# Dilated attention scores: the low part of q over 128 rows, and the sink mixer's outputs parked in DRAM

## The chip, the cores and the metric

The kernel runs on one core of one Trainium2 chip. The metric is the time of one execution on the device in microseconds; the time of a version is the median of several runs. The profile is that of one execution, taken by the hardware profiler.

## What is computed

Two layers of a decoder over 512 tokens of width 1024. Each layer projects the normalized row once and feeds three causal token mixers: sparse attention (A: an indexer scores the keys, the best 128 are kept), dilated window attention (B), and sliding-window attention with sinks (C). Their outputs are gated, merged and projected, and a feed-forward block of width 4096 follows. The part that the change touches is B's scores and C's outputs:

```
for g, (window, dil) in enumerate(((128, 1), (512, 4), (2048, 16))):     # B, four heads in each group
    pos    = t[:, None] - dil * arange(window // dil + 1)[None, :]
    logits = einsum('bqhd,bqkhd->bqhk', q_g, k_g[:, pos]) * scale         # masked where pos < 0
    ...                                                                   # softmax, values, merged by denominators
o_c    = sink_window_attention(...)                                       # C, eight heads, 128 tokens back
merged = g0 * (o_a @ w_a) + g1 * (o_b @ w_b) + g2 * (o_c @ w_c)
```

Everything is float32. Heads have 64 dimensions, tokens come in four blocks of 128.

## The kernel before

TensorE multiplies in a reduced float32 form, so each operand x is split into a high part (x rounded to that form) and a low part (x minus the high part), and a product is the sum of three: high by high, high by low, low by high. `mm3` (lines 287 to 289) issues these three for the big products. `load` fetches a stretch of weights on SP's queue into a buffer `raw`, ScalarE casts the high part (line 263), VectorE or GpSimd subtracts for the low part (line 264).

In the scores the three products are folded into two matmuls, because a head has 64 dimensions and the array 128 rows. In mixers A and C `stack_q` puts the high part of q on 64 rows and the low part on the other 64; `dup_k` holds k twice, and `qk` (lines 368 and 369) multiplies over 128 rows both times. Mixer B stores it the other way: for each head `e` of a pair the tile of k holds the high part on the head's own 64 rows and the low part on the other 64; the tile of q holds the high part on both. So one matmul over 128 rows (line 701) gives high by high plus high by low, and a second one over the head's own 64 rows only (line 702) adds low by high. That low part of q (`ql`) takes one row half per head, two heads in one tile.

`b_project(pr)` projects v, q and k for a pair of heads of each of the three groups, in chunks of 384 columns, token block by token block. After the rope turn a deferred step `post` (the post, below) transposes the block on TensorE and evacuates it: for each head ScalarE copies the high part to the own half (line 660) and, for q, to the other half (line 663), then VectorE subtracts for the low part (line 666). There is one such pair of copies for group 0 (64x128) and one for groups 1 and 2 (64x256).

`b_attend(pr)` then runs eight units of scores, softmax and values as a pipeline: two heads, two kinds (group 0, or groups 1 and 2), two halves of the token blocks. A unit of the second kind has eight matmuls of 128 columns in its scores. One of the first kind has four: two of 128 and two of 256 columns in the first half of the tokens, four of 256 in the second. Line 727 on VectorE takes the row's extreme, line 732 on ScalarE the exponential.

In each layer the program orders the work thus: projections for A and C, the indexer's scores, `c_attend` side by side with gate products, `b_project(0)`, `b_attend(0)` side by side with gate products, `b_project(1)`, `b_attend(1)` in the same way, A's projection with the merge of B, `a_attend` with the rest of the gates, then `split_o` (all mixer outputs into high and low part), `branches`, the output projection and the feed-forward block. The steps of the top-k selection on VectorE (lines 508 and 509) are spread over the dilated mixer's stages. The gates' values are stored in DRAM when they are made (line 849) and fetched in `branches`.

The framework sets the final order on each engine: its planner goes through the instructions with an estimate of each one's cost and of when its inputs are due, and places a tile in a buffer when one is free. Big tiles of 4 KB per partition share the pool `arena` of 15 buffers. The outputs `oC` of C occupy two of them from `c_attend` to `split_o`.

Of the kernel before, what the change touches and what calls it, by code (L numbers as in the profile page):

```python
# [22 lines left out]
P = 128  # L23
T = 512
# [19 lines left out]
class Trunk:  # L44
# [81 lines left out]
        return inv  # L126

    def rope_turns(self, pos, inv):
        """negated angles of rope, reduced to turns in [-0.5, 0.5], and the same a quarter turn on;
        a step for each vector instruction"""  # L130
        v = self.nc.vector
        n = NT * 32
        keep = lambda dt=F32: self.arena([P, n], dt)
        posf = self.cp.tile([P, NT], F32, name="posf")
        yield v.tensor_copy(posf, pos)
        ang = keep()
        yield v.tensor_tensor(
            ang.rearrange("p (b d) -> p b d", d=32), inv.unsqueeze(1).to_broadcast([P, NT, 32]),
            posf.unsqueeze(2).to_broadcast([P, NT, 32]), op=ALU.mult)
        whole = keep(I32)  # L140
        yield v.tensor_copy(whole, ang)
        parts = self.arena([P, 4, n], I32)
        yield v.tensor_scalar(parts[:, 0, :], whole, 255, None, op0=ALU.bitwise_and)
        for j in (1, 2):
            yield v.tensor_scalar(parts[:, j, :], whole, 8 * j, 255, op0=ALU.arith_shift_right, op1=ALU.bitwise_and)
        yield v.tensor_scalar(parts[:, 3, :], whole, 24, None, op0=ALU.arith_shift_right)
        pf = self.arena([P, 4, n], F32)
        yield v.tensor_copy(pf, parts)
        wf = keep()
        yield v.tensor_copy(wf, whole)  # L150
        s1, s2 = keep(), keep()
        yield v.tensor_tensor(s2, ang, wf, op=ALU.subtract)
        yield v.tensor_scalar(s2, s2, float(np.float32(1 / (2 * math.pi))), None, op0=ALU.mult)
        inv2pi = Fraction(INV_2PI_NUM, 1 << 160)
        for j in range(4):
            c = (inv2pi * (1 << (8 * j))) % 1
            c1 = Fraction(round(c * (1 << 14)), 1 << 14)
            p = pf[:, j, :]
            if j == 0:
                yield v.tensor_scalar(s1, p, float(c1), None, op0=ALU.mult)  # L160
            else:
                yield v.scalar_tensor_tensor(s1, p, float(c1), s1, op0=ALU.mult, op1=ALU.add)
            yield v.scalar_tensor_tensor(s2, p, float(np.float32(float(c - c1))), s2, op0=ALU.mult, op1=ALU.add)
        near = keep()

        def turn_back(x):
            """x -> (nearest whole number) - x"""
            yield v.tensor_scalar(near, x, ROUND, None, op0=ALU.add)
            yield v.scalar_tensor_tensor(x, near, ROUND, x, op0=ALU.subtract, op1=ALU.subtract)

        yield from turn_back(s1)
        yield v.tensor_tensor(s1, s2, s1, op=ALU.subtract)
        yield from turn_back(s1)
        q = keep()
        yield v.tensor_scalar(near, s1, 0.25, None, op0=ALU.is_gt)
        yield v.scalar_tensor_tensor(q, s1, 0.25, near, op0=ALU.add, op1=ALU.subtract)
        self.turns = (s1, q)
# [10 lines left out]
            nc.scalar.activation(self.cos[:, :, h * 32 : h * 32 + 32], s2v, AF.Sin, scale=two_pi)  # L188

    def square_sum(self, h, half):  # L190
        """sum over a half of the row, with half of D * EPS"""
        nc = self.nc
        ss = self.st([P, 1], "st")
        junk = self.st([P, T], "sg")
        nc.scalar.activation(junk, h[:, half * T : half * T + T], AF.Square, accum_out=ss)
        if half == 0:
            nc.vector.tensor_scalar(ss, ss, D * EPS, None, op0=ALU.add)
        return ss
# [9 lines left out]
        return rs  # L208

    def norm(self, h, gb, ss0=None):  # L210
        """yields the halves of the normalized row"""
        nc = self.nc
        rs = self.inv_rms(h, ss0)
        yield
        for half in range(2):
            u = self.st([P, T], "t")
            s = slice(half * T, half * T + T)
            nc.vector.scalar_tensor_tensor(u, h[:, s], rs, gb[:, s], op0=ALU.mult, op1=ALU.mult)
            yield u
# [21 lines left out]
        yield  # L241

    def norm_T(self, *args):
        """the normalization up to its transposes; those wait for `catch_up`"""
        g = self.norm_T_steps(*args, late=True)
        next(g)
        next(g)
        self.late.append(g)
# [4 lines left out]
        self.late = []  # L253

    def load(self, parts, width, lo_eng=None):
        """parts: list of (dst slice fn, src ap); one staged tile of `width` f32 columns."""
        nc = self.nc
        raw = self.st([P, 1024], "raw")
        for dst, src in parts:
            nc.sync.dma_start(dst(raw), src)  # L260
        hi = self.st([P, 1024], "hi", F32R)
        lo = self.st([P, 1024], "lo", F32R)
        nc.scalar.copy(hi[:, :width], raw[:, :width])  # L263
        (lo_eng or nc.vector).tensor_tensor(lo[:, :width], raw[:, :width], f32(hi[:, :width]), op=ALU.subtract)  # L264
        return hi, lo

    def load_chunk(self, w, k0, nk, cols, pool_tiles=()):
        """rows k0*128.. of w, column runs `cols` [(start, n)] side by side -> per k (hi, lo) APs."""
        n = sum(c for _, c in cols)
        out = []  # L270
        for k in range(k0, k0 + nk, 2):
# [36 lines left out]
            yield  # L308

    def rope(self, src, tb, nh, dup=1):  # L310
        """src [P, nh*64] (psum or sbuf) -> sbuf tile [P, nh, dup, 64]"""
        nc = self.nc
        x = src.rearrange("p (h two d) -> p h two d", two=2, d=32)
        c = self.cos[:, tb : tb + 1, :].to_broadcast([P, nh, 64])
# [22 lines left out]
        return ps  # L337

    def stack_q(self, roped, nh):
        """[tok, nh*64] -> [P = (hi 64 | lo 64), nh, tok]"""  # L340
        nc = self.nc
        q = self.arena([P, 8, P])[:, :nh, :]
        np_ = nh // 2
        ps = self.transposes(roped, np_)
        for e in range(2):
            src = ps[e * 64 : e * 64 + 64, :np_, :]
            hi = q[0:64, e::2, :]
            nc.scalar.copy(hi, src)
            nc.vector.tensor_tensor(q[64:128, e::2, :], src, f32(hi), op=ALU.subtract)  # L349
        return q  # L350

    def dup_k(self, roped, n, tb, dst):
        """roped [tok, n*128] (each key head twice) -> dst[i][P, hi/lo, 512]"""
        nc = self.nc
        ps = self.transposes(roped, n)
        for i in range(n):
# [12 lines left out]
        nc.tensor.matmul(out, q, k[:, 1, c0 : c0 + n], start=False, stop=True)  # L369

    def softmax(self, ps_list, masks, n, init=None, sink=None, normalize=True):
        """each psum [P, n] -> exp in an sbuf tile [P, heads, n]"""
        nc = self.nc
        nh = len(ps_list)
        lg = self.st([P, 1024], "lg")
# [31 lines left out]
        return pt  # L407

    def av_shared(self, pts, vs, n):
        """sum over blocks of stacked v^T P^T -> psum [P, n]; rows 64.. are the low parts"""  # L410
        nc = self.nc
        ps = self.psum([P, T], "o")
        for i, (pt, v) in enumerate(zip(pts, vs)):
# [2 lines left out]
        return ps  # L416

    def put_o(self, ps, heads, qb, oT):
        """oT(pair) -> [P, 512] f32 AP; heads: list in psum column order"""
        nc = self.nc  # L420
        n = len(heads) * P
        t = self.st([P, T], "t")
# [2 lines left out]
            o = oT(hd // 2)[(hd % 2) * 64 : (hd % 2) * 64 + 64, qb * P : (qb + 1) * P]  # L425
            nc.vector.tensor_tensor(o, ps[0:64, i * P : (i + 1) * P], t[0:64, i * P : (i + 1) * P], op=ALU.add)

# [1 line left out]
    def idx_project(self, uT, w, wk=None):  # L429
        self.iq = {}  # L430

# [136 lines left out]

        yield from pipeline([unit(qb, h0) for qb in range(NT) for h0 in (0, 3)])

# [1 line left out]
    def c_project(self, uT, w):  # L572
        self.cq = {}

# [10 lines left out]
    def c_attend(self, l):  # L585
# [41 lines left out]
            return logits, rest, transpose, values  # L627

        yield from pipeline([unit(qb, g) for qb in range(NT) for g in range(2)])

# [1 line left out]
    def b_alloc(self):  # L632
        self.stat_n = self.st([P, 2, NT, 4], "bst", bufs=6)
        self.stat_c = self.st([P, 2, NT, 4], "bst", bufs=6)
# [1 line left out]
    def b_project(self, uT, w, pr):  # L636
        nc = self.nc
        res = {}
        for which, off in (("v", OFF_BV), ("q", OFF_BQ), ("k", OFF_BK)):
            cols = [(off + g * 256 + pr * P, P) for g in range(3)]  # L640
            if which != "v":
# [1 line left out]
                both = [self.arena([P, 2, T]) for _ in range(2)]  # L643
                res[which] = [[full[:, e, :] for e in range(2)]] + [[both[e][:, g, :] for e in range(2)] for g in range(2)]
                if which == "q":
                    lo0, lo12 = self.arena([P, 2, T])[:, 0, :], self.arena([P, 2, T])
                    res["ql"] = [lo0, lo12[:, 0, :], lo12[:, 1, :]]

                def ev(tb, ps, which=which, full=full, both=both):
                    r = self.rope(ps[:, :384], tb, 6)  # L650
# [3 lines left out]
                    def post():  # L654
                        pt = self.transposes(r, 3)
                        src = pt[:, 0, :], pt[:, 1:3, :].rearrange("p g (j r) -> p g r j", r=4)
                        for e in range(2):
# [3 lines left out]
                            if which == "q":  # L661
                                for x, dst in zip(src, (full[:, e, s], classes(both[e]))):
                                    nc.scalar.copy(dst[other], x[own])
                            low = (lo0[own, s], classes(lo12)[own]) if which == "q" else (full[other, e, s], classes(both[e])[other])
                            for x, dst, lo in zip(src, (full[:, e, s], classes(both[e])), low):
                                nc.vector.tensor_tensor(lo, x[own], f32(dst[own]), op=ALU.subtract)

                    return post
            else:
# [19 lines left out]
    def b_attend(self, pr):  # L689
# [6 lines left out]
        def unit(e, kind, b2, po):  # L696
# [2 lines left out]

            def qk(out, g, qs, ks):  # L700
                nc.tensor.matmul(out, r["q"][g][e][:, qs], r["k"][g][e][:, ks], start=True, stop=False)  # L701
                nc.tensor.matmul(out, r["ql"][g][ep, qs], r["k"][g][e][ep, ks], start=False, stop=True)  # L702

            st = self.stat_n if kind == 0 else self.stat_c
            bs = (2 * b2, 2 * b2 + 1)
# [115 lines left out]
            v.tensor_tensor(self.oB[:, pr, :], t, t2, op=ALU.add)  # L821
            yield

# [1 line left out]
    def split_o(self):  # L825
        nc = self.nc
        out = []
# [154 lines left out]


def pipeline(units):
    """units' stages drawn side by side, each unit one stage behind the one before it"""
    depth = len(units[0])
    for r in range(len(units) + depth - 1):
        for s in reversed(range(depth)):
# [7 lines left out]


def merge(*streams):
    """(generator, its number of steps) pairs, drawn evenly side by side"""
    order = sorted(((i + 0.5) / n, j) for j, (_, n) in enumerate(streams) for i in range(n))  # L1000
    for _, j in order:
        next(streams[j][0], None)
# [1 line left out]
def build(tr):  # L1004
# [53 lines left out]
    for l in range(DEPTH):  # L1058
# [29 lines left out]
        run(ba)  # L1088
        run(tk)
        merge((ap, 5), (tr.b_merge(), 5))  # L1090
        merge((tr.a_attend(), 11), (gt, 12))
        run(gt)
        tr.split_o()
        for f in range(NK):
# [60 lines left out]
```

## Time and profile before

| | |
|---|---|
| median of 3 runs | 1804.34 us (1802.95 to 1808.7) |
| span of the profiled execution | 1805.4 us |
| TensorE busy | 1755.3 us, 97% |
| VectorE busy | 1048.1 us, 58% |
| ScalarE busy | 817.9 us, 45% |
| mean granted TensorE clock | 0.995 of full speed |
| DMA | 186.32 MB, 103 GB/s on average |

The span reaches from the first to the last instruction of the profiled execution; no time of that execution beside its span is given. Busy shares are averages over stages with different limits. A matmul's recorded duration holds its latency, and successive ones overlap, so how fast they follow one another is read from their start times.

### The profile page before, as it was taken

What the parts mean: (1) busy time and instruction counts of PE and PEld (TensorE: products, weight loads), DVE (VectorE), ACT (ScalarE), POOL (GpSimd) and SP (SyncE); (2) the same over time, 40 slices, a digit from 0 to 9 for tenths busy, and PEclk for the clock granted to TensorE, in tenths of its full rate; (3) what the DMA queues carried; (4) which work ended last, traced back from release to release, by engine and by line L of the source; (5) the groups of instructions that cost most, each with busy time, mean ns of one, the idle gap of its engine ahead of it and who ended that gap; (6) DMA issues with size and microseconds to landing.
All of it is one profiled execution on the core that took longest, in us unless ns stands there. A gap on an engine that the chain in (4) does not pass through costs nothing.

```text
span 1805.4 us, 24273 instructions
## 1 busy us (share of the span) xinstructions
PE 1755.3 (97%) x8832; PEld 1483.2 (82%) x8832; DVE 1048.1 (58%) x2200; ACT 817.9 (45%) x1681; POOL 187.5 (10%) x163
## 2 busy tenths in 40 slices
PE   7999999999999999999999999999999999999998
PEld 6789889777879888888887798988788798888886
DVE  7986748667855333333488866596688443333333
ACT  5484544437434333424355845345383342424142
POOL 3310211221000000000021112021210000000000
PEclk9999999999999999999999999999999999999999
DMA  5323333331762322222332243332228422233321
GB/s 179 71 67 99 82 100 85 97 81 51 218 227 74 113 94 93 94 94 93 113 111 64 63 123 88 100 80 75 74 74 263 152 94 93 96 103 104 105 95 47
DMA packets 184344, 186.32 MB, mean 103 GB/s; under 512 B 16672, under 2 KB 125216, under 8 KB 184224
## 3 DMA queue, kind: packets, MB, share of 16 engines
q1 hardware_dynamic: 184224, 184.77, 34.3%
q8 instruction: 69, 1.13, 0.3%
q14 instruction: 51, 0.42, 0.1%
HBM read 165.82 MB, written 16.78 MB: 101 GB/s over the span
## 4 chain that ended last, share of the span: by engine, by line
PE 84%; DVE 9%; ACT 3%; issue 3%; DMA 1%; POOL 0%; SPq 0%; POOLq 0%; ACTq 0%; DVEq 0%
PE psg L287 24%; PE psg L289 24%; PE psg L288 24%; DVE t L324 2%; PE pst L336 1%; PE psl L702 1%; PE psl L701 1%; DVE a L492 1%; DVE a L349 1%; ACT lg L385 1%; PE pst L739 1%; PE pst L560 1%; PE psl L368 1%; ACT hi L263 1%; DVE t L320 1%
## 5 line engine op out<-in xcount | busy, mean ns | idle before, releaser
L263 ACT CAST hi<-raw 128x1024 fp32r<-128x1024 f32 (+3 forms) x320 | 295.6, 930 | 280.1 <-PE psg L289 221.2
L287 PE MATMUL psg<-uT,hi 128*128 128x512 f32 (+1 forms) x896 | 349.7, 390 | 0.0
L288 PE MATMUL psg<-uT,hi 128*128 128x512 f32 (+1 forms) x896 | 345.6, 386 | 0.0
L289 PE MATMUL psg<-uT,lo 128*128 128x512 f32 (+1 forms) x896 | 344.9, 385 | 0.0
L264 DVE TENSOR_TENSOR lo<-raw,hi 128x1024 fp32r<-128x1024 f32 (+4 forms) x237 | 267.8, 1140 | 115.9 <-ACT hi L263 110.6
L287 PE MATMUL psg<-hi,a 128*128 128x512 f32 x640 | 249.8, 390 | 1.8 <-ACT a L876 1.8
L289 PE MATMUL psg<-hi,a 128*128 128x512 f32 x640 | 249.3, 390 | 0.0
L288 PE MATMUL psg<-lo,a 128*128 128x512 f32 x640 | 249.0, 389 | 0.0
L264 POOL TENSOR_TENSOR lo<-raw,hi 128x768 fp32r<-128x768 f32 (+2 forms) x83 | 160.9, 1954 | 615.6 <-ACT hi L263 502.7
L288 PE MATMUL psg<-lo,uT 128*128 128x384 f32 (+2 forms) x624 | 219.1, 351 | 2.3 <-POOL lo L264 1.2
L287 PE MATMUL psg<-hi,uT 128*128 128x384 f32 (+2 forms) x624 | 220.9, 355 | 0.1
L289 PE MATMUL psg<-hi,uT 128*128 128x384 f32 (+2 forms) x624 | 218.5, 350 | 0.0
L287 PEld LDWEIGHTS psg<-uT,hi 128*128 128x128 f32 x896 | 169.2, 189 | 32.5 <-issue 0.7
L289 PEld LDWEIGHTS psg<-uT,lo 128*128 128x128 f32 x896 | 169.4, 189 | 31.8
L288 PEld LDWEIGHTS psg<-uT,hi 128*128 128x128 f32 x896 | 169.4, 189 | 29.4 <-issue 0.7
L947 DVE TENSOR_TENSOR a<-a,psg 128x512 f32<-128x512 f32 x64 | 43.9, 685 | 176.5 <-PE psg L289 176.5
L287 PEld LDWEIGHTS psg<-hi,a 128*128 128x128 f32 x640 | 120.1, 188 | 27.4 <-ACT a L876 2.6
L289 PEld LDWEIGHTS psg<-hi,a 128*128 128x128 f32 x640 | 120.1, 188 | 25.9 <-DVE a L877 0.9
L288 PEld LDWEIGHTS psg<-lo,a 128*128 128x128 f32 x640 | 120.2, 188 | 24.7
L910 DVE TENSOR_TENSOR a<-t,a 128x512 fp32r<-128x512 f32 x64 | 44.2, 690 | 153.3 <-ACT a L909 153.3
L288 PEld LDWEIGHTS psg<-lo,uT 128*128 128x128 f32 x624 | 117.7, 189 | 10.4 <-DVE lo L264 2.2
L287 PEld LDWEIGHTS psg<-hi,uT 128*128 128x128 f32 x624 | 117.7, 189 | 7.2 <-ACT uT L239 0.5
(195 smaller groups left out, 2502.0 us busy)
## 6 DMA issues: line engine op xcount, KB each, us to landing
raw<-in_w_in_dram SPq DMA_DIRECT2D x336, 128.0 KB, 2.8
raw<-in_w_up_dram SPq DMA_DIRECT2D x64, 512.0 KB, 4.8
raw<-in_w_down_dram SPq DMA_DIRECT2D x64, 512.0 KB, 4.8
raw<-in_w_in_dram SPq DMA_DIRECT2D x24, 512.0 KB, 4.7
sgd<-sg SPq DMA_DIRECT2D x48, 256.0 KB, 2.0
sg<-sgd SPq DMA_DIRECT2D x48, 256.0 KB, 3.7
raw<-in_w_o_dram SPq DMA_DIRECT2D x16, 512.0 KB, 4.1
a<-in_x_dram SPq DMA_DIRECT2D x8, 512.0 KB, 8.4
```

Source lines behind the costliest of these rows:

```text
L263: nc.scalar.copy(hi[:, :width], raw[:, :width])
L264: (lo_eng or nc.vector).tensor_tensor(lo[:, :width], raw[:, :width], f32(hi[:, :width]), op=ALU.subtract)
L287: nc.tensor.matmul(out, lh, rh, start=start, stop=False)
L288: nc.tensor.matmul(out, lh, rl, start=False, stop=False)
L289: nc.tensor.matmul(out, ll, rh, start=False, stop=stop)
L320: nc.vector.tensor_tensor(v1, src.rearrange("p (h d) -> p h d", d=64), c, op=ALU.mult)
L324: self.last_dve = nc.vector.tensor_tensor(v1, v1, v2, op=ALU.add)
L336: self.nc.tensor.transpose(ps[:, i, :], src[:, i * P : (i + 1) * P], self.ident)
L349: nc.vector.tensor_tensor(q[64:128, e::2, :], src, f32(hi), op=ALU.subtract)
L368: nc.tensor.matmul(out, q, k[:, 0, c0 : c0 + n], start=True, stop=False)
L910: nc.vector.tensor_tensor(a[:, 1, :], r, f32(a[:, 0, :]), op=ALU.subtract)
L947: nc.vector.tensor_tensor(hc, hc, ps, op=ALU.add)
```

## The change

The low part of q is stored like the high part, on both halves of the rows: `ql` now has a tile for each head (three tiles of the arena instead of two), VectorE subtracts into the head's own half as before, and ScalarE copies the result into the other half. The second matmul of `qk` in B contracts over all 128 rows of k's tile. So it also adds low by low, which was left out before.

At the end of `c_attend` the two tiles of `oC` are stored in DRAM on SP's queue. `c_reload`, called after five of the eleven steps of `a_attend`, takes two tiles of the arena anew and fetches them. The gates' steps are drawn in two halves of six around it.

```diff
@@ c_attend, at its end, and a new function
         yield from pipeline([unit(qb, g) for qb in range(NT) for g in range(2)])
+        self.oCd = []
+        for g in range(2):
+            d = self.dr.tile([P, 2, T], F32, name=self.uid("oCd"))
+            nc.sync.dma_start(d, self.oC[g])
+            self.oCd.append(d)
+
+    def c_reload(self):
+        self.oC = [self.arena([P, 2, T], F32) for _ in range(2)]
+        for g in range(2):
+            self.nc.sync.dma_start(self.oC[g], self.oCd[g])
@@ b_project
                 if which == "q":
-                    lo0, lo12 = self.arena([P, 2, T])[:, 0, :], self.arena([P, 2, T])
-                    res["ql"] = [lo0, lo12[:, 0, :], lo12[:, 1, :]]
+                    lfull = self.arena([P, 2, T])
+                    lboth = [self.arena([P, 2, T]) for _ in range(2)]
+                    res["ql"] = [[lfull[:, e, :] for e in range(2)]] + [[lboth[e][:, g, :] for e in range(2)] for g in range(2)]
...
-                            low = (lo0[own, s], classes(lo12)[own]) if which == "q" else (full[other, e, s], classes(both[e])[other])
+                            if which == "q":
+                                low = lfull[:, e, s], classes(lboth[e])
+                            else:
+                                low = full[:, e, s], classes(both[e])
                             for x, dst, lo in zip(src, (full[:, e, s], classes(both[e])), low):
-                                nc.vector.tensor_tensor(lo, x[own], f32(dst[own]), op=ALU.subtract)
+                                at = own if which == "q" else other
+                                nc.vector.tensor_tensor(lo[at], x[own], f32(dst[own]), op=ALU.subtract)
+                                if which == "q":
+                                    nc.scalar.copy(lo[other], f32(lo[own]))
@@ b_attend
                 nc.tensor.matmul(out, r["q"][g][e][:, qs], r["k"][g][e][:, ks], start=True, stop=False)
-                nc.tensor.matmul(out, r["ql"][g][ep, qs], r["k"][g][e][ep, ks], start=False, stop=True)
+                nc.tensor.matmul(out, r["ql"][g][e][:, qs], r["k"][g][e][:, ks], start=False, stop=True)
@@ build
-        merge((tr.a_attend(), 11), (gt, 12))
+        aa = tr.a_attend()
+        merge((aa, 5), (gt, 6))
+        tr.c_reload()
+        merge((aa, 6), (gt, 6))
```

The rest of the diff empties comments and docstrings.

## Rows read from the trace of the kernel before

**Rows 1.** The page, busy time: engine, us, share of the span, instructions.

```profile
PE 1755.3 (97%) x8832; PEld 1483.2 (82%) x8832; DVE 1048.1 (58%) x2200; ACT 817.9 (45%) x1681; POOL 187.5 (10%) x163
```

**Rows 2.** Stretches: bounds, length, busy time (instructions) per engine, clock, DMA share, GB/s.

```profile
core 0: us, PE busy (x) PEld busy (x) DVE busy (x) ACT busy (x) POOL busy (x), PEclk, DMA share, GB/s
172.00:190.00 18.00, 17.70 (x107) 17.30 (x106) 15.95 (x41) 11.51 (x33) 4.36 (x2) 1.00 0.40 96
...
206.00:240.00 34.00, 34.00 (x194) 27.12 (x194) 19.84 (x65) 16.73 (x43) 7.59 (x5) 1.00 0.39 102
...
300.00:316.00 16.00, 15.31 (x88) 14.30 (x86) 15.05 (x33) 6.43 (x19) 2.64 (x2) 1.00 0.18 45
316.00:332.00 16.00, 14.36 (x71) 11.21 (x72) 15.54 (x44) 7.12 (x22) 4.96 (x3) 1.00 0.37 100
332.00:366.00 34.00, 34.00 (x207) 27.64 (x207) 18.86 (x53) 16.93 (x41) 5.48 (x3) 1.00 0.28 82
...
412.00:450.00 38.00, 37.26 (x205) 31.47 (x204) 30.10 (x100) 30.16 (x75) 5.54 (x3) 1.00 0.17 53
...
1206.00:1222.00 16.00, 14.45 (x65) 11.15 (x66) 14.13 (x39) 6.48 (x20) 4.87 (x3) 0.89 0.39 101
```

**Rows 3.** Timeline of TensorE, dilated mixer: start, duration, line, rows*columns of weights, operand.

```profile
210.50 0.38 PE L702 MATMUL psl<-a,a 64*128 64x256 f32 x1
...
211.13 0.38 PE L702 MATMUL psl<-a,a 64*128 64x256 f32 x1
...
214.55 0.22 PE L288 MATMUL pso<-pt,a 128*64 128x128 f32 x1
214.61 0.22 PE L289 MATMUL pso<-pt,a 128*64 128x128 f32 x1
...
215.64 0.32 PE L702 MATMUL psl<-a,a 64*128 64x128 f32 x1
...
217.16 0.32 PE L702 MATMUL psl<-a,a 64*128 64x128 f32 x1
```

**Rows 4.** Timeline of TensorE: scores of the sink mixer, then of the indexer.

```profile
109.62 0.28 PE L369 MATMUL psl<-a,a 128*128 128x256 f32 x1
...
110.33 0.28 PE L369 MATMUL psl<-a,a 128*128 128x256 f32 x1
...
986.23 0.28 PE L369 MATMUL psl<-a,a 128*128 128x128 f32 x1
...
986.90 0.27 PE L369 MATMUL psl<-a,a 128*128 128x128 f32 x1
```

**Rows 5.** Groups by line and shape: count, busy us, mean ns, idle before.

```profile
L660 ACT CAST a<-pst 64x256 fp32r<-64x256 f32 x64 | 23.4, 366 | 0.1
L702 PE MATMUL psl<-a,a 64*128 64x128 f32 x72 | 23.4, 326 | 0.0
...
L660 ACT CAST a<-pst 64x128 fp32r<-64x128 f32 x64 | 16.7, 261 | 70.4 <-PE pst L336 41.3 <-DVE a L666 28.5
...
L831 ACT CAST a<-a 128x512 fp32r<-128x512 f32 x18 | 9.8, 617 | 0.0
...
L702 PE MATMUL psl<-a,a 64*128 64x256 f32 x24 | 9.2, 381 | 0.0
```

**Rows 6.** Waits: who for whom, us in total, times, longest.

```profile
ACT a L660 <- DVE a L666: 28.5, 21, 2.8
```

**Rows 7.** The chain that ended last, second projection of q: start, us, what.

```profile
300.74 0.62 DVE a L666 x2
301.39 0.53 ACT a L660 x2
```

**Rows 8.** DMA issues by line: count, KB each, median us to landing.

```profile
h<-a SPq DMA_DIRECT2D x4, 512.0 KB, 2.6
a<-h SPq DMA_DIRECT2D x4, 512.0 KB, 7.2
```

**Rows 9.** Stretches of the second attend's start, columns as in rows 2.

```profile
324.00:330.00 6.00, 6.00 (x36) 4.84 (x35) 5.86 (x17) 2.61 (x8) 0.00 (x0) 1.00 0.13 49
```

## What the change does to the time: prediction

> **What bounds the kernel now.** I read the page first: TensorE is busy for 97% of the span, ScalarE for 45% [rows 1]. That average hides which stage waits for what, so I cut the first layer into stages with the view of stretches [rows 2]. The reader is to see three kinds of stage. While the dilated mixer attends (206 to 240 and 332 to 366 us), TensorE is busy 34.0 of 34 us, so whatever is taken from TensorE there shortens the kernel. Between them, where the second pair of heads is projected, VectorE leads: 15.05 of 16 us from 300 to 316, and 15.54 of 16 from 316 to 332, with TensorE at 14.36. In the first projection of q (172 to 190) TensorE leads with 17.70 of 18, VectorE has 15.95, ScalarE 11.51.
>
> A busy TensorE does not say how fast its matmuls follow one another, so the third view is its own timeline, read as distance from start to start. In the dilated scores [rows 3] the pair of lines 701 and 702 alternates: 701 contracts over 128 rows, 702 over 64. From the 702 at 215.64 to the 702 at 217.16 lie six starts: (217.16 - 215.64)/6 = 0.253 us for a matmul of 128 columns. From 210.50 to 211.13 lie two: 0.315 us for 256 columns. The scores of the other mixers use the same two-matmul form, but with 128 rows in both [rows 4]: (986.90 - 986.23)/6 = 0.112 us for 128 columns, and (110.33 - 109.62)/6 = 0.118 us for 256. So the dilated scores pay about 0.14 to 0.2 us more per matmul. The clock is not the reason: it is granted at 1.00, the 2.4 GHz level, in the stretch that holds 210 to 217 [rows 2], and 256 columns in 0.118 us can't be had at 1.2 GHz, where they alone would take 0.213. What is left as the difference is the change between 64 and 128 rows.
>
> **The change part by part: the scores.** 192 matmuls are touched: 72 + 24 of line 702 [rows 5], and as many of line 701. After the edit both contract over 128 rows, as in rows 4. At those distances the saving is 144 x (0.253 - 0.112) = 20.3 us for 128 columns and 48 x (0.315 - 0.118) = 9.5 us for 256, together 29.8 us, on the engine that sets the time there. Nearest rows bound it: nothing, if the distance comes from something else than the rows (rival below), and 29.8 us, which I take in full, because the form after is exactly that of rows 4: fp32r, 128 partitions, two matmuls into one bank.
>
> The rows alone give this; a page differs within itself on it. The Trainium skill, TensorEngine Tiling (Array Packing), Key Properties, says that a change of tiling mode, not only of the tile, drains TensorE. Going from 128 to 64 rows and back is such a change, and the 0.253 against 0.112 us agrees. TensorE: Matmul & The Clock Gate, in its step-by-step part on loading the stationary operand, says that the time follows the columns and that the row count doesn't matter; by that rule alone the sum would have no gain here, and it is the first rival.
>
> **The low part of q.** Line 666 keeps its count on VectorE; what is new are ScalarE copies into the other half: for each of 2 layers, 2 pairs of heads, 4 token blocks and 2 heads one of 64x128 and one of 64x256, 32 each. ScalarE's own copies of that size from PSUM (line 660) take 261 and 366 ns [rows 5]; these read SBUF, and an SBUF copy of twice the columns, line 831, takes 617 ns [rows 5], so nothing suggests a much higher price. 32 x (0.261 + 0.366) = 20.1 us of ScalarE, that is 5.0 us per projection of q. In the first projection ScalarE has 18 - 11.51 = 6.5 us free [rows 2], so the work fits, but barely.
>
> More than the work it is the order that counts. The new copy waits for VectorE's subtraction, and behind it on ScalarE stand the next head's copies (line 660), then casts of weights (line 263), for which VectorE's low parts and TensorE wait in turn. The wait for VectorE's subtraction at this spot is there already: ScalarE waits for line 666 before line 660, 21 times, 28.5 us [rows 6], 1.36 us each. The chain shows why: two subtractions to 301.39, then at once line 660 of the next head [rows 7]. There the first new copy lies beside the second subtraction; the second copy is serial. I price a post (the deferred step that copies one token block of q) at two such copies, 2 x 0.37 = 0.74 us, when it is on the chain. In the second projection, which VectorE leads, I count two posts per layer: 2 x 2 x 0.74 = 3.0 us. In the first, where TensorE leads, only the last: 2 x 0.74 = 1.5 us. Sum 4.5 us. Bounds: 0, as all may lie under TensorE's gemm, and 20.1 us if every copy is serial. I take a value near the lower end, because TensorE leads two of the four projections. Without cover this edit costs the whole 20.1 us and the waits on top.
>
> **What the saving meets.** At the start of the second attend VectorE is nearly full: 5.86 of 6 us from 324 to 330 [rows 9]. TensorE can't pull ahead there. Two of the eight groups of scores lie in that opening, one of four matmuls of mixed width (about 0.7 us saved) and one of four of 256 columns (4 x 0.197 = 0.8 us). I take these 1.5 us as lost in both layers, 3.0 us; bounds 0 and that. Elsewhere VectorE has room (the top-k steps are its work there), and the saving stays.
>
> **Parking.** Per layer two stores and two loads of 512 KB on SP's queue. The kernel's own transfers of this size land in 2.6 us as a store and 7.2 us as a load [rows 8]. The store waits for the last output of the sink mixer and stands ahead of the weight loads of q; the weights of v, issued earlier, still feed TensorE then. The loads are issued halfway through sparse attention; that stretch (412 to 450) has a DMA share of 0.17 [rows 2], and the outputs are first needed at its end, some 19 us later. I take 0. If the cover were gone, the loads would show with 2 x 2 x 7.2 = 28.8 us.
>
> The parking frees two arena buffers and the wider low part takes one more, so buffers get no scarcer, and no new wait for one is counted.
>
> Sum: 1805.4 - 29.8 + 4.5 + 3.0 = 1783.1 us on the profiled span. The profile names no time of its own beside the span; the span stands 1.1 us above the median of the runs (1804.34), so the median becomes **1782 us**. The median's spread (1802.95 to 1808.7) suggests that 0.3%, 5.4 us, is about what can be told from no change.
>
> **Rivals.**
>
> *Rows don't matter, faster it isn't.* The distance of 0.253 us comes from another trait, say two different stationary tiles in turn. Against: the value matmuls 288 and 289 alternate such tiles and start 0.06 us apart [rows 3]. For: no row shows this same pair at 128 rows. Then only costs stay: 1804.3 + 0 to 7.5 = 1804 to 1812 us.
>
> *VectorE and ScalarE take it back.* The rounds of the attends become bound by exponentials, top-k and copies, and nearly all posts go serial: 1804.3 - 29.8 + 20.1 + 3.0 = 1798 us at worst, 1790 at the near end. For: VectorE at 15.54 of 16 us. Against: from 332 to 366 VectorE has 18.86 of 34 us.
>
> *Slower: the queue of ScalarE stalls in the posts of q.* Each of the 32 pairs of new copies makes ScalarE wait for VectorE as long as it does now, 1.36 us, and adds its 0.63 us; weight casts behind it come late and TensorE stands. All on the path: 32 x (1.36 + 0.63) = 64 us, 1804.3 - 29.8 + 64 = 1838 us. It decides once a pair costs over 29.8/32 = 0.93 us on the path. For: VectorE's queue there holds rope and top-k steps ahead of the subtraction. Against: ScalarE already waits for the same subtraction, and TensorE has work in hand. A TensorE idle of that sort also lowers the clock: 0.89 granted from 1206 to 1222 us [rows 2], after the projection that VectorE leads.
>
> **How the numbers follow.** Forecast, 1773 to 1790 us: 0.63. More than that, below 1773, if free buffers shorten the stretch that VectorE leads: 0.06. Taken back, 1790 to 1799: 0.13. Rows don't matter: 0.06, half of it within 5.4 us. ScalarE stalls, above 1810: 0.07. A new order of the instructions by the planner, which knows other costs than the chip, eats it without one place to name, 1799 to 1810: 0.05. The range of 1772 to 1799 leaves out about 2 in 10. Faster than 1798.9: 0.63 + 0.06 + 0.13 = 0.82. Within 0.3%: 0.03 + 0.05 = 0.08. Slower: 0.03 + 0.07 = 0.10.
>
> **What would show it.** Lines 701 and 702 about 0.112 and 0.118 us apart, both at 128 rows; each group of eight about 1.1 us shorter. The new ScalarE copies: 32 each, near 261 and 366 ns, with line 660's wait for line 666 grown or replaced by a wait for the copies. The stretch from the first scores of an attend to the last 7 us shorter, the projection of the second pair about 1.5 us longer. Stores and loads of the parked outputs: four each, nobody waiting for them. Wrong would make me: a distance still near 0.25 us; TensorE idle before the posts or the attends; SP waiting long at the store.

## The result and the profile after

The changed kernel takes 1778.8 us (median of 4 runs, 1778.47 to 1779.97), the kernel before 1806.24 us beside it (4 runs, 1802.95 to 1808.7). The ratio is 0.9854, with a 95% interval from 0.9838 to 0.9869 (ratios, here and below, are estimated from the single runs and need not equal the quotient of the medians). The profiled spans are 1777.3 and 1805.4 us, 28.1 us apart.

The page, busy time per engine, answers to [rows 1]:

```profile
PE 1726.1 (97%) x8832; PEld 1468.4 (83%) x8832; DVE 1044.0 (59%) x2200; ACT 837.4 (47%) x1745; POOL 185.3 (10%) x163
```

ScalarE has 64 instructions and 19.5 us more, TensorE 29.2 us less with the same count. The timeline of TensorE in the first attend answers to [rows 3]; line 719 is the former 702, and square brackets give TensorE's idle time before a row and what ended it:

```profile
210.96 0.36 PE L718 MATMUL psl<-a,a 128*128 128x256 f32 x1
211.16 0.28 PE L719 MATMUL psl<-a,a 128*128 128x256 f32 x1
211.28 0.28 PE L718 MATMUL psl<-a,a 128*128 128x256 f32 x1
211.40 0.28 PE L719 MATMUL psl<-a,a 128*128 128x256 f32 x1
212.34 0.44 PE L756 MATMUL pst<-ident,lg 128*128 128x128 f32 x2 [0.67 <-ACT lg L749]
...
216.28 0.30 PE L718 MATMUL psl<-a,a 128*128 128x128 f32 x1
216.43 0.27 PE L719 MATMUL psl<-a,a 128*128 128x128 f32 x1
...
217.09 0.28 PE L719 MATMUL psl<-a,a 128*128 128x128 f32 x1
217.21 0.45 PE L287 MATMUL psg<-uT,hi 128*128 128x512 f32 x1
```

From 216.43 to 217.09 lie six starts, 0.110 us each, where it was 0.253; 256 columns follow one another after 0.12 us instead of 0.315. These are about the distances of [rows 4]. New is the 0.67 us at 212.34: TensorE now waits there for the first exponentials.

Groups by line and shape, the new copies, answer to [rows 5]:

```profile
L683 ACT CAST a<-a 64x256 fp32r<-64x256 f32 x32 | 12.9, 403 | 0.5
...
L683 ACT CAST a<-a 64x128 fp32r<-64x128 f32 x32 | 9.5, 298 | 7.1 <-DVE a L681 6.7
```

They take 298 and 403 ns, 37 more than copies of the same size from PSUM.

Waits, answering to [rows 6], and the parked outputs' stores (line 633) and loads (639) in SP's own queue:

```profile
ACT a L671 <- DVE a L681: 19.8, 12, 2.8
...
ACT a L683 <- DVE a L681: 6.7, 14, 0.9
```

```profile
SPq L633 <- DVE a L625: 2.8, 2, 1.4
...
SPq L639 <- PE pst L560: 0.8, 2, 0.4
```

The wait of ScalarE for the subtraction has split: 28.5 us before one line became 19.8 before one and 6.7 before the other. SP waited 1.4 us for the last output of the sink mixer, twice.

DMA issues, KB each and median us to landing, answer to [rows 8]:

```profile
oCd<-a SPq DMA_DIRECT2D x4, 512.0 KB, 3.1
...
a<-oCd SPq DMA_DIRECT2D x4, 512.0 KB, 4.5
```

Where the 28 us come from is read best from the lengths of the stages, from the first start of a line to the first start of the next stage's line (lines of the kernel before: sink mixer 615, v 675, scores 701, sparse attention 560, branches 872 from its first to its last; the end of layer 0 is counted from the first 906). The kernels of the experiments stand beside them:

| us, layer 0 / layer 1 | before | after | E1 | E2 | E3 | E4 | E6 |
|---|---|---|---|---|---|---|---|
| start, and end of layer 0, to the sink mixer | 104.5 / 422.6 | 105.2 / 420.5 | 104.3 / 421.6 | 104.0 / 421.6 | 104.5 / 422.7 | 103.7 / 420.4 | 104.1 / 421.5 |
| first projection | 51.9 / 51.9 | 52.5 / 52.5 | 52.5 / 52.5 | 51.9 / 51.9 | 51.9 / 51.9 | 51.9 / 51.9 | 51.9 / 51.9 |
| first attend, first to last score | 41.3 / 41.3 | 35.0 / 34.9 | 41.3 / 41.3 | 36.3 / 36.3 | 41.2 / 41.3 | 35.0 / 35.0 | 35.0 / 35.0 |
| second projection | 56.4 / 57.6 | 56.6 / 55.4 | 55.4 / 55.4 | 57.7 / 57.7 | 56.4 / 57.7 | 56.4 / 55.6 | 52.2 / 52.3 |
| second attend, first to last score | 41.3 / 41.6 | 34.5 / 35.2 | 41.3 / 41.3 | 36.4 / 36.4 | 41.3 / 41.5 | 35.2 / 35.2 | 34.9 / 34.9 |
| last score to sparse attention | 48.9 / 48.9 | 48.6 / 48.6 | 48.9 / 48.9 | 49.2 / 49.2 | 48.9 / 48.9 | 48.5 / 48.5 | 50.1 / 50.0 |
| branches | 48.5 / 48.3 | 49.2 / 49.6 | 50.5 / 51.1 | 48.1 / 48.3 | 48.4 / 48.6 | 49.2 / 48.6 | 48.2 / 49.2 |

The four attends are 25.8 us shorter (6.3 + 6.8 + 6.3 + 6.4), and what follows each another 0.3 us, 1.2 in all. The first projections are 1.3 us longer, the second ones together 2.1 us shorter. The end of layer 0 is 2.2 us shorter, the branches 2.0 us longer, the start 0.7 longer, the very end 0.9 shorter. The other stages that the table leaves out moved by less than 0.1 us each. The sum is -28.2 us. The 0.9 us at the very end stand in every kernel with the parking, E3 too, and not in E2; why the parking shortens it stays open.

### The profile page after: what moved, and what is told of

Its sections match the earlier page's. It is cut to its first block, busy times and chain, and to the rows that moved or that the text cites. A ratio compares the mean times of both kernels' runs of the same rounds, so it can differ in the third digit from the quotient of the medians.

```text
span 1777.3 us, 24351 instructions
## 1 busy us (share of the span) xinstructions
PE 1726.1 (97%) x8832; PEld 1468.4 (83%) x8832; DVE 1044.0 (59%) x2200; ACT 837.4 (47%) x1745; POOL 185.3 (10%) x163
## 4 chain that ended last, share of the span: by engine, by line
PE 80%; DVE 11%; issue 3%; ACT 2%; DMA 2%; POOL 0%; SPq 0%; POOLq 0%; DVEq 0%; ACTq 0%
PE psg L287 23%; PE psg L289 23%; PE psg L288 23%; PE pst L336 1%; DMA sg<-sgd 1%; DVE t L324 1%; DVE a L681 1%; DVE a L492 1%; PE psl L368 1%; DVE lo L264 1%; DVE a L349 1%; DVE t L320 1%; PE psl L369 1%; PE pst L560 1%; DVE t L321 1%
## 5 line engine op out<-in xcount | busy, mean ns | idle before, releaser
L289 PEld LDWEIGHTS psg<-hi,a 128*128 128x128 f32 x640 | 120.1, 188 | 25.8 <-DVE a L894 0.9
```

The source lines that it names most:

```text
L289: nc.tensor.matmul(out, ll, rh, start=False, stop=stop)
```

## The experiments

My theory after the result: what costs is each change between matmuls over 128 rows and over 64. Rivals: a matmul over 64 rows is slow by itself, or something else in the new layout made the scores dense.

**E1: the changed kernel, 64 rows again.** All copies and the parking stay.

```diff
-                nc.tensor.matmul(out, r["ql"][g][e][:, qs], r["k"][g][e][:, ks], start=False, stop=True)
+                nc.tensor.matmul(out, r["ql"][g][e][ep, qs], r["k"][g][e][ep, ks], start=False, stop=True)
```

> The changed kernel with all its copies and its parking, but the second matmul of the dilated scores contracts over the head's own 64 rows again. Theory (the alternation of 128 and 64 rows costs the distance): from start to start 0.253 us for 128 columns and 0.315 us for 256 again, each attend 41 to 42 us from first to last score instead of 35, time 1804 to 1809 us. Rival (something else in the new layout, such as a tile for each head, made the matmuls denser): distance stays at 0.112 us, attends stay at 35 us, time near 1779 us.

Measured: 1805.62 us against 1806.23 for the kernel before, ratio 1.0001 (0.9989 to 1.0013). The timeline of TensorE in its first attend:

```profile
216.16 0.32 PE L719 MATMUL psl<-a,a 64*128 64x128 f32 x1
...
217.69 0.32 PE L719 MATMUL psl<-a,a 64*128 64x128 f32 x1
```

Six starts in 1.53 us, 0.255 each, and all attends 41.3 us long again. So the whole gain hangs on this one operand slice; the layout, the copies and the parking give none of it.

**E2: the kernel before, grouped by rows.** In each unit the matmuls over 128 rows come first (only the very first opens the bank), then those over 64; the lines left out collect a unit's parts in `todo`.

```diff
-            def qk(out, g, qs, ks):
-                nc.tensor.matmul(out, r["q"][g][e][:, qs], r["k"][g][e][:, ks], start=True, stop=False)
-                nc.tensor.matmul(out, r["ql"][g][ep, qs], r["k"][g][e][ep, ks], start=False, stop=True)
+            def qk(todo):
+                for i, (out, g, qs, ks) in enumerate(todo):
+                    nc.tensor.matmul(out, r["q"][g][e][:, qs], r["k"][g][e][:, ks], start=i == 0, stop=False)
+                for i, (out, g, qs, ks) in enumerate(todo):
+                    nc.tensor.matmul(out, r["ql"][g][ep, qs], r["k"][g][e][ep, ks], start=False, stop=i == len(todo) - 1)
...
```

> The kernel before, but in each unit all matmuls over 128 rows are issued first and then all over 64 rows, so that the row count changes twice in a unit instead of 8 or 4 times. Theory (each change of the row count costs, not the 64 rows): inside both runs of equal rows 0.112 us for 128 columns and 0.118 us for 256; 128 of the 192 costly distances go, 128 x 0.15 = 19 us, time about 1786 us. Rival (a matmul over 64 rows is slow by itself): the 64-row run keeps 0.25 us from start to start, and only the 128-row run gets dense, about 1790 us with the difference plain in the start times. Rival (rows don't matter): 1805 us.

Measured: 1786.62 us, ratio 0.9899 (0.9877 to 0.992). A unit of eight on TensorE's timeline, here merged by line (start and length of a run of four):

```profile
214.44 0.64 PE L702 MATMUL psl<-a,a 128*128 128x128 f32 x4
215.01 0.66 PE L704 MATMUL psl<-a,a 64*128 64x128 f32 x4
215.60 0.50 PE L287 MATMUL psg<-uT,hi 128*128 128x512 f32 x1
```

A run over 64 rows is as dense as one over 128: four in 0.59 and 0.57 us up to the next line's start. The fourth of each run starts here:

```profile
214.80 0.27 PE L702 MATMUL psl<-a,a 128*128 128x128 f32 x1
...
215.40 0.27 PE L704 MATMUL psl<-a,a 64*128 64x128 f32 x1
```

Its three inner distances take 0.36 us over 128 rows and 0.39 us over 64, and the step across a change 0.21 us (214.80 to 215.01) and 0.20 us (215.40 to 215.60). Against 4 x 0.112 = 0.45 us a run of four with its change costs 0.12 and 0.14 us more, about what a single matmul with its change pays in the kernel before (0.253 - 0.112 = 0.14). So 64 rows aren't slow; the change is, in either direction. The 0.118 us expected for 256 columns did not show: runs of that width are two matmuls long, and their one distance is 0.20 us over 128 rows, behind a transpose, and 0.22 us over 64, behind a change. The time lies where this theory put it.

**E3: the kernel before with the parking alone.** Edit: the stores, `c_reload` and its call, as in the change.

> The kernel before with the parking of the sink mixer's outputs alone. Theory (transfers are hidden, and the changed kernel's branches stage got 0.7 and 1.3 us longer from something else): time within 3 us of 1805, branches stage as before. Rival (the parking shortens the second projection by its two freed buffers, which got 1 us shorter in the changed kernel where 1.5 us more were forecast): the second projection about 1 us shorter in both layers. Rival (the parking costs): branches stage 0.7 to 1.3 us longer per layer, time 1806 to 1809 us.

Measured: 1804.2 us, ratio 0.9993 (0.9979 to 1.0006); every stage of the table within 0.3 us of before, and the very end 0.9 us shorter. The transfers are hidden, and the freed buffers alone shorten no stage of the table. Whether the wide low part would run without the parking wasn't tried: in the second attend 17 tiles would be live (2 outputs of C, the scores of the top-k, 2 outputs of B, 12 of q, k and v) in an arena of 15.

**E4: zeros instead of copies.** GpSimd fills the other half; low by low is left out again.

```diff
+                    for e in range(2):
+                        other = slice(64 - e * 64, 128 - e * 64)
+                        self.nc.gpsimd.memset(f32(lfull[other, e, :]), 0.0)
+                        self.nc.gpsimd.memset(f32(lboth[e][other, :, :]), 0.0)
...
-                                if which == "q":
-                                    nc.scalar.copy(lo[other], f32(lo[own]))
```

> The changed kernel without the 64 new ScalarE copies: the other half of the low part of q is set to zero by GpSimd, so low by low is left out, as in the kernel before. Theory (the copies lengthen the first projection by 0.7 us per layer and cost nothing else): 1777 to 1778.5 us. Rival (the copies' price was hidden by a gain elsewhere, and they are worth the forecast 4.5 us or more): 1774 us or less. Rival (GpSimd's fills slow VectorE or come late before the posts): over 1779 us.

Measured: 1777.44 us, ratio 0.9851 (0.9829 to 0.9873): not to be told from the changed kernel. The stages say more: the first projection is 51.9 us again, as before, in both layers. So the copies cost there 0.6 us per layer. GpSimd's fills, 16 of them, take 0.52 and 0.95 us each.

**E5: the changed kernel again.** No edit.

> The changed kernel once more, on the chip of the next three. Theory (the lengths of the branches stage, 49 to 51 us in the kernels so far, differ with the DMA's timing and not with the edit): its time again 1777 to 1781 us, and its branches stages change by up to 1 us against the first profile. Rival: the branches stages keep 49.2 and 49.6 us to 0.1 us.

Measured: 1777.15 us, ratio 0.9841 (0.9826 to 0.9855). Branches 49.6 and 49.1 us, against 49.2 and 49.6 in the first profile, so they move by half a microsecond without an edit. The start moved by 1.4 us, from 105.2 to 103.8: the stretch from 86 to 100 us was granted 0.76 of the clock in the first profile and 0.88 in this one, as in the kernel before. The changed kernel first, then the repeat (columns as in [rows 2]):

```profile
86.00:100.00 14.00, 10.67 (x49) 8.76 (x49) 11.57 (x21) 7.24 (x17) 4.08 (x2) 0.76 0.41 95
```

```profile
86.00:100.00 14.00, 10.70 (x54) 8.88 (x55) 12.30 (x26) 7.55 (x19) 3.34 (x2) 0.88 0.38 86
```

**E6: VectorE's load moved.** E4, and nine of the fourteen top-k steps that the program drew with the second projection are drawn with the attends.

```diff
-        merge((ba, 10), (gt, 12), (tk, 12))
+        merge((ba, 10), (gt, 12), (tk, 16))
         draw(bp, 1)
         run(ba)
-        merge((bp, 15), (tk, 14))
+        merge((bp, 15), (tk, 5))
         ba, ap = tr.b_attend(1), tr.a_project(uT, w)
-        merge((ba, 10), (gt, 12), (tk, 12))
+        merge((ba, 10), (gt, 12), (tk, 16))
```

> Zeros in the other half instead of copies, and nine of the fourteen top-k steps of the second projection moved into the two attends. Theory (VectorE leads the second projection, and TensorE has 4.5 us less there than in the first): that stage shrinks from 56.4 to 52 to 54 us in both layers, time 1769 to 1774 us. Rival (something else holds TensorE there, or the steps take their time back in the attends): no change against 1777.4 us.

Measured: 1771.97 us (1771.31 to 1772.1), ratio 0.9809 (0.9793 to 0.9826). This is the fastest version here, 5.2 us under the repeat of the changed kernel on the same chip. Stretches of the second projection in layer 0, the changed kernel first, then E6:

```profile
273.00:293.00 20.00, 18.82 (x112) 18.16 (x111) 17.66 (x37) 13.16 (x37) 3.89 (x2) 1.00 0.38 90
293.00:309.00 16.00, 15.73 (x93) 15.06 (x91) 15.01 (x34) 8.76 (x28) 2.06 (x3) 1.00 0.29 70
```

```profile
272.00:292.00 20.00, 19.34 (x116) 18.95 (x115) 16.62 (x37) 11.53 (x33) 4.96 (x4) 1.00 0.46 108
292.00:308.00 16.00, 15.86 (x92) 14.97 (x92) 11.30 (x27) 7.81 (x22) 5.67 (x3) 1.00 0.22 50
```

In the trace three top-k steps run in that stage instead of eight. VectorE falls from 15.01 to 11.30 of 16 us, and the stage from 56.4 (E4) to 52.2 us, the length of the first projection. VectorE did lead there. 1.5 us per layer come back between the second attend and sparse attention, where the last steps of the top-k now end later (8.3 us behind the last score instead of 2.4) and TensorE waits 1.2 us for a low part on GpSimd, as it did not before.

**E7: low parts of the dilated weights on VectorE alone.** E4, and `gemm_tok(uT, w, cols, range(NT), ev, None, ())` in `b_project`.

> Zeros in the other half instead of copies, and in the dilated projections all low parts of weights on VectorE, none on GpSimd. In the profiles some additions of the rope turn take 2.2 us instead of 0.56 while GpSimd subtracts. Theory (these long ones cost VectorE more than GpSimd saves it: 1.6 against 1.1 us a chunk): second projection 1 to 2 us shorter, time 1774 to 1777 us. Rival (VectorE loses by the added work): the second projection 1 to 2 us longer per layer, 1779 to 1782 us.

Measured: 1783.28 us, ratio 0.9873 (0.9859 to 0.9888), a miss. The second projection gained little or nothing (55.9 and 56.9 us against 56.4 and 55.6), and stages outside it grew: the first projection from 51.9 to 53.1 us, the sink mixer ahead of it by 1.6 and 1.0 us.

**E8: E6 and E7 together.**

> Both edits of the two kernels ahead together, zeros instead of copies. If each gain is VectorE's time in the second projection, they add up until TensorE leads there, at 52 us: 1768 to 1773 us. If one of them gains nothing, the time is that of the other alone.

Measured: 1777.69 us, ratio 0.9845 (0.9826 to 0.9863). The second projection takes 53.1 us, more than E6's 52.2, so the gains don't add up; E7's edit only costs. Why it costs stays open.

## Why the prediction was right, point by point

**The scores.** Forecast 29.8 us, measured 27.0 (25.8 in the attends, 1.2 just behind them). Cause and place are shown: E1 takes the gain back with the slice alone, E2 takes about two thirds of it by order alone. The term was 2.8 us too large. In three of the four attends TensorE now waits for the first exponentials, 0.67, 0.66 and 0.29 us, together 1.6. The other 1.2 are a size: in the eight groups of four matmuls over 256 columns the first distance, behind a transpose, is 0.20 us (210.96 to 211.16), not the 0.118 that the sum used, and in the eight groups of mixed width the first over 256 columns is about 0.17 us.

**The copies.** In the first projections 1.5 us were forecast and 1.3 measured, and E4 shows that they are the copies'. In the second ones 3.0 us were forecast, and none came: this is the step that failed. Where the granted clock is 1.00 throughout, the stage takes 56.4 us before, with the parking alone (E3) and with zeros (E4), each in layer 0, and 55.4 in the changed kernel (layer 1) and in both layers of E1. I had counted two posts per layer as on the chain because the chain of before ran through them; the planner drew another order for the kernels with copies, on ScalarE and VectorE, while E4 has that of before on both. TensorE's starts in that stage, counted from its first, agree to 0.001 us between the kernel before and those with copies up to one spot, and behind it lie 1.01 us earlier to the stage's end. TensorE's timeline at the spot, before, then after:

```profile
295.70 0.45 PE L288 MATMUL psg<-lo,uT 128*128 128x384 f32 x1 [0.57 <-DVE lo L264]
...
297.88 0.52 PE L336 MATMUL pst<-ident,t 128*128 128x128 f32 x3 [1.56 <-DVE t L324]
```

```profile
291.10 0.44 PE L288 MATMUL psg<-lo,uT 128*128 128x384 f32 x1 [1.18 <-DVE lo L264]
...
291.66 0.52 PE L336 MATMUL pst<-ident,t 128*128 128x128 f32 x3
```

TensorE waits 0.6 us longer for a low part of weights, and the 1.56 us for the rope's addition (line 324) are gone: 1.0 us less. VectorE's addition, before, then after:

```profile
295.56 2.17 DVE L324 TENSOR_TENSOR t<-t,t 128x384 f32<-128x384 f32 x1
```

```profile
290.97 0.55 DVE L324 TENSOR_TENSOR t<-t,t 128x384 f32<-128x384 f32 x1
```

Before, GpSimd made two low parts of weights in a row there (292.97 to 297.31), and the addition took 2.17 us beside the second. In the changed kernel the new copies stand ahead of a weight cast on ScalarE, GpSimd waits 0.72 us for that cast, its second low part starts only with the addition (290.95), and the addition takes 0.55 us. E1 waits as the changed kernel does, E3 and E4 as the kernel before. One of the two layers has a lower clock in either profile (the last section), so the 2.1 us of the table are about twice this 1.0. All this is read from the traces; what the copies cost in the old order no run shows. (E4's layer 1, 55.6 us, has a lower clock and lacks another wait for such an addition, 0.15 us instead of 2.1 before the last transposes, so it is left out.)

**The opening of the second attend.** 3.0 us were forecast as lost. The waits come to 1.6 us, about half, and the place was wrong: 1.33 us of them lie in the two first attends. The second attend of layer 0 lost nothing (6.8 us saved), but there the granted clock had just fallen (0.89 from 311 to 327 us), and TensorE took 0.85 us for its first group of scores instead of 0.46 in layer 1. Where the clock was 1.00 at that opening (layer 1 of the changed kernel, both layers of E4 and E6), a wait of 0.3 us stands there; in both layers of E5, at 0.89, none does. VectorE's 5.86 of 6 us [rows 9] were mostly top-k steps, which are not the scores' own work.

**Parking.** Forecast 0, measured 0 but for the 0.9 us at the very end (E3). The loads landed in 4.5 us, long before their use.

**What no term had.** The end of layer 0 is 2.2 us shorter without any edit there; the last section tells why. The branches are 2.0 us longer, of which E5 moves half a microsecond by itself per stage; in E1 they took 2.0 and 2.8 us more than before. There SP's loads of gates and weights set the pace on the chain of the changed kernel, and no run here separates the transfers' timing from their order. That stays open.

On the profiled span the forecast of 1783.1 us came out 5.8 us too high. The scores less the opening came out, 26.8 us forecast and 27.0 measured, in part by luck, since the matmuls saved 1.2 us less and the waits took 1.4 us less than forecast; the copies were mis-sized, 4.5 forecast against -0.8 measured (1.3 - 2.1); what no term had is -0.4 us together (0.7 - 2.2 + 2.0 - 0.9). The median of 1782 us is only 3.2 us too high, and this too is luck: the runs lie 1.5 us above this span and not 1.1 below it. Of the rivals, that rows don't matter fell with E1 and E2, that VectorE and ScalarE take it back fell with the attends, which kept 25.8 us, and that ScalarE stalls fell with the table: a pair of copies had to cost 0.93 us on the path, and 16 of them cost 1.3 us in the first projections. The Trainium skill's TensorEngine Tiling (Array Packing), Key Properties, says that changing the tiling mode drains TensorE. E2 agrees, and gives the price in this kernel: 0.20 to 0.21 us across a change instead of 0.11 us, and 0.12 to 0.14 us in all for a run with its change. The Trainium skill's TensorE: Matmul & The Clock Gate says, in its step-by-step part on loading the stationary operand, that the row count doesn't matter. The starts within a run of equal rows agree (E2: three distances in 0.36 and 0.39 us), those across a change don't.

## What to carry to other kernels

Read a bound TensorE by the distance between starts, by shape, and compare with another place of the kernel that has the same columns: a matmul over fewer rows may cost nothing by itself and still cost its neighbours. Where it alternates with full-height ones, group by height (E2, 20 us without one more instruction) or fill the rows with zeros or copies (27 us). Where a second engine leads between two stages that TensorE bounds, its elastic work belongs into the stages where it has room (E6).

## What was not expected of the hardware

The same wait of TensorE was followed by a lower clock in one execution and not in the other. At the start of layer 1 TensorE waits 2.67 us for the same addition, before and after; TensorE's timeline before, then after:

```profile
979.70 0.88 PE L336 MATMUL pst<-ident,t 128*128 128x128 f32 x3 [2.67 <-DVE t L324]
```

```profile
968.31 0.52 PE L336 MATMUL pst<-ident,t 128*128 128x128 f32 x3 [2.67 <-DVE t L324]
```

Stretches around it, before, then after (columns as in [rows 2]):

```profile
978.00:990.00 12.00, 10.30 (x47) 9.25 (x48) 9.44 (x22) 5.64 (x17) 1.00 (x1) 0.72 0.30 69
```

```profile
964.00:976.00 12.00, 9.33 (x53) 7.28 (x52) 11.60 (x24) 6.14 (x18) 3.62 (x2) 1.00 0.45 108
```

Before, part of the stretch ran at the lower of the two levels, 1.2 GHz (granted 0.72 on average), and the stage to the sink mixer took 422.6 us; after, 2.4 GHz throughout and 420.5 us. All ten profiles show this wait, 2.65 to 2.70 us long. Over 12 us around it the clock was granted at 1.00 in the changed kernel, E4 and E5, where the stage takes 420.4 to 420.5 us, at 0.86 in E1, E2, E6 and E7 with 421.5 to 421.6 us, and at 0.72 before, in E3 and in E8 with 422.6 to 422.7 us: the stage follows the clock and not the edit. In the changed kernel layer 0's second projection has such a fall (0.89 from 311 to 327 us) and layer 1's has none, in the kernel before it is the other way round [rows 2], and E5 shows 1.4 us at the start of one and the same kernel. So single stages of two profiles differ by 1 to 2 us with no edit behind it.

The change of 128 weight columns to 64 between scores, transposes and values showed no such price: the value matmuls start 0.06 us apart right behind gate products, before [rows 3] and after.
